# Joining two value parts in one product, and moving tiles and sparse steps between the stages of a decoder layer

## The chip, the cores and the metric

The kernel runs on one core of a Trainium2 chip. The metric is the device time of one execution in microseconds; shorter is better. TensorE is called PE, VectorE DVE, ScalarE ACT, GpSimd POOL and SyncE SP, as in the profile.

## The reference, cut to what matters

One decoder layer for 256 tokens of 1024 columns in float32: conditioned norm, an input projection with a retention group and a sparse-attention group, an output projection, and then an expert stage, in which the change lies:

```python
q = (hblk @ w_q).reshape(B, TB, PEER_HEADS, 2, PEER_DHALF)
s = jnp.einsum('btphd,phnd->btphn', q, subkeys).astype(jnp.float32)
v, i = lax.top_k(s, PEER_TOPK)
cand = (v[..., 0, :, None] + v[..., 1, None, :]).reshape(B, TB, PEER_HEADS, PEER_TOPK * PEER_TOPK)
cidx = (i[..., 0, :, None] * PEER_NKEYS + i[..., 1, None, :]).reshape(B, TB, PEER_HEADS, PEER_TOPK * PEER_TOPK)
tv, tj = lax.top_k(cand, PEER_TOPK)
eidx = jnp.take_along_axis(cidx, tj, axis=-1)
w = jax.nn.softmax(tv, axis=-1)
u = w_down[eidx]
a = jax.nn.gelu(jnp.einsum('btd,btpkd->btpk', hblk, u).astype(jnp.float32))
vv = w_up[eidx]
return jnp.einsum('btpk,btpkd->btd', (w * a).astype(hblk.dtype), vv)
```

Each token chooses 16 of 16384 experts for each of 8 heads, 128 expert numbers and weights in all. An expert is a row of `w_down` and a row of `w_up`.

## The kernel before, in words

The expert stage treats two sets of tokens differently. For the last 192 tokens (TD) it computes the whole 16384 x 192 table: 128 **down tiles** (one block of 128 experts each) give the Gelu of the down products, a **W part** writes the weights that the tokens give to the experts, and 128 **up units** multiply the weighted table with `w_up`. For the first 64 tokens (TS) it gathers the chosen rows: 64 **sparse steps** fetch 128 rows of `w_down` each with an indirect DMA on POOL (tile `row`, 0.5 MB) and take dot products on DVE, and 64 more fetch rows of `w_up` and add them up in `accS` (`sparse_gen`, lines 1028 to 1063).

The order of work is written out by the loop at line 1255. It walks a list `seq` of units: 16 query units (`wq`), then 128 down units; after the W part the rest of the down units alternate with up units, and the other up units follow. Beside the units run two generators:

- `gen` is first `top_gen` (line 941), which builds the expert lists on DVE, and then `w_gen` (line 1065). Each piece of it costs credits at its `yield`; each unit brings credits: CQ = 1.7 for a query unit, CT = 1.1 for a down unit while the lists are built (phase "top"), CD = 1.15 in the W part. So the credits decide how many tiles lie beside the lists and beside the W part. The lists cost 1.1 for each of 32 first-stage lists and 2 x (2 x 1.1 + 8 x 2.1 + 1.3 + 1.0) for the second stage of the two token blocks; the W part costs 1.0 + 0.4 for each of 48 groups. What is unspent is kept, up to 3.
- `spg` is the sparse work. A down unit brings it RD = 0.7 of a step, an up unit RU = 0.45.

A down tile (`down_unit`, line 1098) is done in one of two ways. A **wide** tile is split first (`split`): ACT copies the raw tile to `H` (float32r), DVE subtracts it to `L`, and PE multiplies 8 times `H` with 384 columns and `L` with 192; ACT then copies one half of the PSUM bank to `g` and DVE adds the other half. A **whole** tile goes to PE as plain float32, which the profile counts as 16 products of 192 columns, and needs neither split nor sum. `split_to` (line 1229) chooses: all tiles of phase "top" are whole, and every third one in the W part. In every case ACT then takes the Gelu from PSUM or `g`.

A W group (4 tokens) goes so: DVE compares a table of the token's expert numbers with a counting tile, which gives two one-hot tiles `o0` and `o1` (float16), and multiplies one of them with the weight's high part (`ow0`); ACT multiplies it with the low part, token by token (`ow1`, four instructions). PE adds up two products of 128 columns in one PSUM bank `w` for each token, eight in all, each with its own load of the same one-hot. After the next `yield`, tiles that are done already (`na` of them) are multiplied in place by DVE (`scalar_tensor_tensor`, which reads PSUM), in two halves VL and VH, and for those not yet done ACT copies the weights there, to be multiplied later.

PSUM has two `w` banks, two `dn` and four `acc`. Down tiles take `dn` or `acc` before the up part, and `dn` alone in it, since the up units' sums lie in `acc`. Raw tiles come by SP's queue, four units ahead, in four buffers; a wide tile frees its buffer after the split, a whole one after its products.

On ACT the Exp of the softmax (line 980) stands in `top_gen` once for each token block; the list indices and weights are then turned by PE (transposes at 1002 to 1004) and cast by DVE to the tables that the W part reads.

Of the kernel before, what the change touches and what calls it, by code (L numbers as in the profile page):

```python
# [24 lines left out]
F32 = mybir.dt.float32  # L25
F32R = mybir.dt.float32r
BF = mybir.dt.bfloat16
F16 = mybir.dt.float16
# [27 lines left out]
BLK = 8  # L56
BD = 3
WD = 3
RD = 0.7
RU = 0.45  # L60
EARLY = 5
NF1 = 3
NF2 = 1
FAFTER = False
SPL = 1
CT = 1.1
AFTER = ("top",)
NCAND = 50
CAND = [(0, 0, 1, 16), (16, 1, 2, 8), (24, 2, 3, 5), (29, 3, 4, 4), (33, 4, 5, 3), (36, 5, 8, 2), (42, 8, 16, 1)]
# [2 lines left out]
def build(tc, I, out, dbg=None, stop=None):  # L72
# [868 lines left out]
    def top_gen(sc):  # L941

        for i in range(16):
            while i not in sc:
                yield None
            b = sc.pop(i)
            for tt in range(2):
                top16(b[:, tt, :], tv1[tt][:, i, :], ti1[tt][:, i, :], P, "s2")
                yield 1.1
        for tt in range(2):  # L950
            fi = mk(tk, (P, 8, 2, 16), F32, "fi", bufs=2)
            V.tensor_copy(fi, ti1[tt].rearrange("p (a b) c -> p a b c", b=2))
            V.tensor_scalar(fi[:, :, 0, :], fi[:, :, 0, :], 128.0, None, op0=ALU.mult)
            v4 = tv1[tt].rearrange("p (a b) c -> p a b c", b=2)
            cand = mk(tk, (P, 8, NCAND), F32, "cand", bufs=2)
            cidx = mk(tk, (P, 8, NCAND), F32, "cidx", bufs=2)
            for src, dst in ((v4, cand), (fi, cidx)):
                for o, a0, a1, nb in CAND:
                    n = (a1 - a0) * nb
                    V.tensor_tensor(dst[:, :, o:o + n].rearrange("p h (a b) -> p h a b", b=nb),  # L960
                                    src[:, :, 0, a0:a1, None].to_broadcast([P, 8, a1 - a0, nb]),
                                    src[:, :, 1, None, 0:nb].to_broadcast([P, 8, a1 - a0, nb]), op=ALU.add)
                yield 1.1
            tv = mk(tk, (P, 8, 16), F32, "tv", bufs=2)
            tp = mk(tk, (P, 8, 16), U32, "tp", bufs=2)
            tpf = mk(tk, (P, 8, 16), BF, "tpf", bufs=2)
            ev = mk(tk, (P, 8, 16), F32, "ev", bufs=2)
            for p in range(8):
                top16(cand[:, p, :], tv[:, p, :], tp[:, p, :], NCAND, "s3")
                V.tensor_copy(tpf[:, p, :], tp[:, p, :])  # L970
                oh = mk(tk, (P, NCAND, 16), BF, "oh", bufs=1)
                V.tensor_tensor(oh, ioj, tpf[:, p:p + 1, :].to_broadcast([P, NCAND, 16]), op=ALU.is_equal)
                oe = mk(tk, (P, NCAND, 16), F32, "oe", bufs=2)
                V.tensor_tensor(oe, oh, cidx[:, p, :, None].to_broadcast([P, NCAND, 16]), op=ALU.mult)
                V.tensor_reduce(ev[:, p, :], oe.rearrange("p j k -> p k j"), axis=AX.X, op=ALU.add)
                yield 2.1

            ex = mk(tk, (P, 8, 16), F32, "ex", bufs=2)
            V.tensor_tensor(ex, tv, tv[:, :, 0:1].to_broadcast([P, 8, 16]), op=ALU.subtract)
            S.activation(ex, ex, AF.Exp)  # L980
            sm = mk(tk, (P, 8), F32, "smx", bufs=2)
            V.tensor_reduce(sm, ex, axis=AX.X, op=ALU.add)
            V.reciprocal(sm, sm)
            V.tensor_tensor(ex, ex, sm[:, :, None].to_broadcast([P, 8, 16]), op=ALU.mult)
            ei = mk(tk, (P, P), I32, "ei", bufs=2)
            V.tensor_copy(ei, ev.rearrange("p a b -> p (a b)"))
            e1 = mk(tk, (P, 2, P), I32, "e1", bufs=1)
            V.tensor_scalar(e1[:, 0, :], ei, 7, None, op0=ALU.arith_shift_right)
            V.tensor_scalar(e1[:, 1, :], ei, 127, None, op0=ALU.bitwise_and)
            ef = mk(tk, (P, 2, P), F32, "ef", bufs=1)  # L990
            V.tensor_copy(ef, e1)
            if tt == 0:

                ew = ex.rearrange("p a b -> p (a b)")
                V.tensor_copy(idxS[:TS, :], ei[:TS, :NJ])
                V.tensor_copy(wS[:TS, :], ew[:TS, :NJ])
                G.dma_start(idxS[TS:, :], ei[:TS, NJ:])
                last["G"] = G.dma_start(wS[TS:, :], ew[:TS, NJ:])
                spg.append(sparse_gen())
            yield 1.3  # L1000
            b = bank("w")[:, :3 * P].rearrange("p (a b) -> p a b", a=3)
            PE.transpose(b[:, 0, :], ef[:, 0, :], ident)
            PE.transpose(b[:, 1, :], ef[:, 1, :], ident)
            PE.transpose(b[:, 2, :], ex.rearrange("p a b -> p (a b)"), ident)
            tq = slice(tt * P, (tt + 1) * P)
            S.activation(tab[:, :, tq], b[:, 0:2, :], AF.Copy)
            wt = mk(tk, (P, P), F32, "wt", bufs=1)
            S.activation(wt, b[:, 2, :], AF.Copy, scale=WSC)
            dump(f"e{tt}", ev)
            dump(f"w{tt}", ex)  # L1010

            V.tensor_copy(tabw[:, tq], wt)
            V.tensor_tensor(tabl[:, tq], wt, tabw[:, tq], op=ALU.subtract)
            yield 1.0
# [50 lines left out]
    def w_gen(ohp):  # L1065

        half = NT // 2
        for gi in range(TD // 4):
            v0 = gi * 4
            t0 = TS + v0  # L1070
            oh = []
            for n in (1, 0):
                o = mk(ohp, (P, P, WG), F16, f"o{n}")
                V.tensor_tensor(o, iow, tab[:, n, None, t0:t0 + WG].to_broadcast([P, P, WG]), op=ALU.is_equal)
                oh.append(o)
            ow = [mk(ohp, (P, P, WG), F16, f"ow{n}") for n in range(2)]
            V.tensor_tensor(ow[0], oh[1], tabw[:, None, t0:t0 + WG].to_broadcast([P, P, WG]), op=ALU.mult)
            for t in range(WG):
                S.activation(ow[1][:, :, t], oh[1][:, :, t], AF.Copy, scale=tabl[:, t0 + t:t0 + t + 1])
            b = bank("w").rearrange("p (a b) -> p a b", a=4)  # L1080
            for t in range(WG):
                for n in range(2):
                    mm(b[:, t, :], oh[0][:, :, t], ow[n][:, :, t], n == 0, n == 1)
            yield 1.0
            bv = b.rearrange("p t i -> p i t")
            na = state["na"]
            for i0, buf in ((0, VL), (half, VH[0])):
                a = min(max(na - i0, 0), half)
                o = buf[:, :, v0:v0 + 4]
                if a:  # L1090
                    V.scalar_tensor_tensor(o[:, :a, :], bv[:, i0:i0 + a, :], 1.0 / WSC, o[:, :a, :], op0=ALU.mult,
                                           op1=ALU.mult)
                if a < half:
                    S.activation(o[:, a:, :], bv[:, i0 + a:i0 + half, :], AF.Copy, scale=1.0 / WSC)
            state["t0"] = v0 + 4
            yield 0.4

    def down_unit(n):
        wide = n not in whole
        if wide:  # L1100
            h, l = splits.pop(("down", n))
        else:
            r, _ = raws.pop(("down", n))
        b = bank("dn" if phase == "up" or n % 3 == 2 else "acc")[:, :2 * TD]
        for k in range(KC):
            ks = slice(k * P, (k + 1) * P)
            if wide:
                two = [(b.rearrange("p (a b) -> p a b", a=2), h[:, ks], h2[k // 4][:, k % 4, :, TS:]),
                       (b[:, :TD], l[:, ks], h2H[:, k, TS:])]
                for n_, o in enumerate(two[::-1] if k else two):  # L1110
                    mm(*o, k == 0 and n_ == 0, k == KC - 1 and n_ == 1)
            else:
                mm(b[:, :TD], r[:, ks], h2f[:, k, :], k == 0, k == KC - 1)
        t0 = state["t0"]
        v = vtile(n)
        if t0 or wide:
            g = mk(gt, (P, TD), F32, "g")
        src = b
        if wide:
            S.activation(g, b[:, TD:], AF.Copy)  # L1120
            V.tensor_tensor(g, g, b[:, :TD], op=ALU.add)
            src = g
        if t0 < TD:
            last["U"] = S.activation(v[:, t0:], src[:, t0:TD], AF.Gelu_apprx_tanh)
        if t0:
            S.activation(g[:, :t0], src[:, :t0], AF.Gelu_apprx_tanh)
            last["U"] = V.tensor_tensor(v[:, :t0], v[:, :t0], g[:, :t0], op=ALU.mult)
        state["na"] = n + 1
# [100 lines left out]
    def split_to(i):  # L1229
        while splitted[0] <= i and splitted[0] < len(seq):  # L1230
            u, n = seq[splitted[0]]
            if u == "down" and (phase == "top" or phase == "w" and n % WD == 0):
                whole.add(n)
                splitted[0] += 1
                continue
# [245 lines left out]
```

## Time and profile before

| | |
|---|---|
| median of 3 runs | 967.46 us (966.09 to 971.69) |
| profiled execution, its own time | 963.1 us |
| its span, first to last instruction | 960.9 us |
| PE busy | 905.5 us, 94% |
| DVE busy | 810.4 us, 84% |
| ACT busy | 521.2 us, 54% |
| POOL busy | 224.8 us, 23% |
| DMA | 266.43 MB, mean 277 GB/s |
| mean granted clock of PE | 0.979 |

A row of the profile names an engine, an operation and its tiles as out<-in with partitions x columns; then how often it ran (x), its busy time and the mean ns of one, and the idle time of the engine just before it with what ended it. Products overlap in PE, so that their durations add up to more than the time they take, and the same holds, by some 0.1 us, for DVE and ACT. Nearly all lines of the kernel go through one helper at line 88; the tiles tell the rows apart.

### The profile page before, as it was taken

How to read it: one execution, taken by the hardware profiler on the slowest of the kernel's cores; microseconds unless marked ns; L12 is line 12 of the kernel's file. 1: busy time of each engine (PE TensorE's matmuls, PEld its weight loads, DVE VectorE, ACT ScalarE, POOL GpSimd, SP SyncE). 2: the span in 40 equal slices, each digit the busy share in tenths (PEclk: the TensorE clock that was granted, in tenths of full speed). 3: DMA queues.
4: the chain of work that ended last, by engine and by line, in shares of the span. 5: the costliest groups of instructions: out<-in, count | busy, mean ns of one | idle time of the engine just before them, and what ended most of it. 6: DMA issues, size and time to landing. Idle time of an engine off the chain costs nothing.

```text
span 960.9 us, 15265 instructions
## 1 busy us (share of the span) xinstructions
PE 905.5 (94%) x5198; PEld 797.2 (83%) x5198; DVE 810.4 (84%) x1788; ACT 521.2 (54%) x1151; POOL 224.8 (23%) x172
## 2 busy tenths in 40 slices
PE   7999999999999799999989987899999989999994
PEld 6875667899999799999989986788887867888883
DVE  7988888689998922899998986889988979898887
ACT  7543697344221123778776754556564545555564
POOL 2040000110004200123223312334442425233311
PEclk9999999999999899999999988999999999999998
DMA  9978765354569976778777677899999999899981
GB/s 361 393 283 290 263 220 177 129 158 143 153 207 387 338 227 218 260 264 281 270 257 263 248 255 258 288 321 345 348 351 359 384 352 354 339 337 341 332 290 44
DMA packets 74749, 266.43 MB, mean 277 GB/s; under 512 B 9400, under 2 KB 9712, under 8 KB 74288
## 3 DMA queue, kind: packets, MB, share of 16 engines
q1 hardware_dynamic: 55200, 193.59, 57.5%
q0 software_dynamic: 19328, 71.61, 20.4%
q8 instruction: 41, 0.67, 0.3%
q14 instruction: 36, 0.29, 0.1%
q10 hardware_dynamic: 144, 0.26, 0.1%
HBM read 263.03 MB, written 2.11 MB: 276 GB/s over the span
## 4 chain that ended last, share of the span: by engine, by line
PE 51%; DVE 26%; DMA 8%; ACT 7%; issue 6%; POOL 1%; SPq 0%; DVEq 0%; ACTq 0%; POOLq 0%
PE acc L88 32%; DVE row L88 5%; PE C L88 5%; PE dn L88 4%; PE O L88 4%; DVE L L88 4%; PE S L88 3%; PE T L88 2%; DVE ev L88 2%; DVE o L88 2%; DMA row<-in_downN_dram,idxS 2%; ACT H L88 2%; ACT ow L88 1%; DMA raw<-in_down_dram 1%; DVE VL L88 1%
## 5 line engine op out<-in xcount | busy, mean ns | idle before, releaser
L88 DVE TENSOR_TENSOR L<-raw,H 128x1024 fp32r<-128x1024 f32 x216 | 263.2, 1220 | 41.9 <-ACT H L88 37.3
L88 ACT ACTIVATE H<-raw 128x1024 fp32r<-128x1024 f32 x216 | 228.2, 1058 | 122.2 <-DMA raw<-in_up_dram 73.4
L88 PE MATMUL acc<-H,a 128*128 128x512 f32 (+1 forms) x774 | 269.9, 397 | 4.4 <-DVE a L88 4.3
L88 PE MATMUL acc<-L,a 128*128 128x512 f32 (+1 forms) x515 | 203.4, 395 | 6.7 <-DVE L L88 6.7
L88 PEld LDWEIGHTS acc<-H,a 128*128 128x128 f32 x774 | 149.4, 193 | 39.8 <-DVE a L88 9.6
L1025 POOL DMA_INDIRECT row<-in_up_dram,idxS x64 | 116.2, 1815 | 196.2 <-DVE accS L88 163.8
L88 PE MATMUL acc<-h2f,raw 128*128 128x192 f32 x816 | 139.2, 326 | 0.0
L1025 POOL DMA_INDIRECT row<-in_downN_dram,idxS x64 | 77.5, 1210 | 242.6 <-DVE VH L88 85.4
L88 PEld LDWEIGHTS acc<-h2f,raw 128*128 128x128 f32 x816 | 133.0, 190 | 0.0
L88 PEld LDWEIGHTS acc<-L,a 128*128 128x128 f32 x515 | 99.1, 192 | 26.5 <-DVE L L88 7.1
L88 PE MATMUL dn<-hT,H 128*128 128x384 f32 x328 | 101.8, 367 | 5.4 <-DVE g L88 5.2
L88 PE MATMUL acc<-hT,H 128*128 128x256 f32 (+1 forms) x408 | 98.0, 323 | 3.6 <-ACT g L88 3.6
L88 DVE SCALAR_TENSOR_TENSOR row<-row,h2rep 128x1024 f32<-128x1024 f32 x64 | 77.9, 1218 | 8.8 <-DMA row<-in_downN_dram,idxS 8.6
L88 DVE SCALAR_TENSOR_TENSOR accS<-row,cS,accS 128x1024 f32<-128x1024 f32 x64 | 81.7, 1277 | 2.2 <-DMA row<-in_up_dram,idxS 2.2
L88 PE MATMUL dn<-hT,L 128*128 128x192 f32 x328 | 77.1, 255 | 0.0
L88 ACT ACTIVATE ow<-o,VL 128x128 f16<-128x128 f16 x192 | 74.4, 572 | 4.0 <-DVE o L88 3.4
L88 PEld LDWEIGHTS acc<-hT,H 128*128 128x128 f32 x408 | 69.7, 194 | 3.9 <-ACT g L88 3.9
L88 PE MATMUL acc<-hT,L 128*128 128x192 f32 (+1 forms) x280 | 72.5, 270 | 0.0
L88 PEld LDWEIGHTS dn<-hT,H 128*128 128x128 f32 x328 | 62.5, 191 | 8.5 <-DVE g L88 7.3
L88 PEld LDWEIGHTS dn<-hT,L 128*128 128x128 f32 x328 | 62.8, 193 | 0.7
L88 PE MATMUL w<-ow,o 128*128 128x128 f16 x384 | 53.2, 296 | 4.1 <-DVE ow L88 2.5
L88 PE MATMUL dn<-h2f,raw 128*128 128x192 f32 x272 | 48.5, 333 | 6.3 <-ACT VL L88 6.3
(355 smaller groups left out, 1367.2 us busy)
## 6 DMA issues: line engine op xcount, KB each, us to landing
raw<-in_down_dram SPq DMA_DIRECT2D x128, 512.0 KB, 4.3
raw<-in_up_dram SPq DMA_DIRECT2D x128, 512.0 KB, 6.3
adaraw<-in_wadaT_dram SPq DMA_DIRECT2D x40, 512.0 KB, 6.0
raw<-in_wq_dram SPq DMA_DIRECT2D x16, 512.0 KB, 3.5
raw<-in_win_C_dram SPq DMA_DIRECT2D x12, 512.0 KB, 6.3
rawA<-in_win_A_dram SPq DMA_DIRECT2D x8, 512.0 KB, 6.5
raw<-in_wout_dram SPq DMA_DIRECT2D x8, 512.0 KB, 3.7
VL<-in_wadaT_dram SPq DMA_DIRECT2D x8, 512.0 KB, 7.1
```

The lines of the kernel that those rows point to most:

```text
L88: i = fn(*a, **kw)
L1025: G.indirect_dma_start(r, None, src, bass.IndirectOffsetOnAxis(ap=idxS[:, j:j + 1], axis=0))
```

## The change

The W group loads the one-hot of a token once and multiplies it with both value parts side by side (256 columns), so that the parts stand next to each other in PSUM and not summed; two tokens fill a bank, a group both `w` banks. ACT copies the low part with the scale to a new tile `wl`, DVE adds the scaled high part to it, and the later multiplication reads `wl` in SBUF. CT rises from 1.1 to 1.5, RD from 0.7 to 0.9, and RU falls from 0.45 to 0.3. In the W part two tiles of three are whole where it was one of three, in the up part every other one where it was none, and down tiles of the up part take `dn` and `w` banks in turn. The Exp of the softmax is ordered behind the last down tile's Gelu.

```diff
@@ -56,14 +56,14 @@
 BLK = 8
 BD = 3
 WD = 3
-RD = 0.7
-RU = 0.45
+RD = 0.9
+RU = 0.3
 EARLY = 5
 NF1 = 3
 NF2 = 1
 FAFTER = False
 SPL = 1
-CT = 1.1
+CT = 1.5
 AFTER = ("top",)
 NCAND = 50
 CAND = [(0, 0, 1, 16), (16, 1, 2, 8), (24, 2, 3, 5), (29, 3, 4, 4), (33, 4, 5, 3), (36, 5, 8, 2), (42, 8, 16, 1)]
@@ -977,7 +977,8 @@
 
             ex = mk(tk, (P, 8, 16), F32, "ex", bufs=2)
             V.tensor_tensor(ex, tv, tv[:, :, 0:1].to_broadcast([P, 8, 16]), op=ALU.subtract)
-            S.activation(ex, ex, AF.Exp)
+            with (tc.issue_after(last["U"].ins) if "U" in last else ExitStack()):
+                S.activation(ex, ex, AF.Exp)
             sm = mk(tk, (P, 8), F32, "smx", bufs=2)
             V.tensor_reduce(sm, ex, axis=AX.X, op=ALU.add)
             V.reciprocal(sm, sm)
@@ -1073,25 +1074,32 @@
                 o = mk(ohp, (P, P, WG), F16, f"o{n}")
                 V.tensor_tensor(o, iow, tab[:, n, None, t0:t0 + WG].to_broadcast([P, P, WG]), op=ALU.is_equal)
                 oh.append(o)
-            ow = [mk(ohp, (P, P, WG), F16, f"ow{n}") for n in range(2)]
-            V.tensor_tensor(ow[0], oh[1], tabw[:, None, t0:t0 + WG].to_broadcast([P, P, WG]), op=ALU.mult)
+            ow = mk(ohp, (P, 2, P, WG), F16, "ow")
+            V.tensor_tensor(ow[:, 0], oh[1], tabw[:, None, t0:t0 + WG].to_broadcast([P, P, WG]), op=ALU.mult)
             for t in range(WG):
-                S.activation(ow[1][:, :, t], oh[1][:, :, t], AF.Copy, scale=tabl[:, t0 + t:t0 + t + 1])
-            b = bank("w").rearrange("p (a b) -> p a b", a=4)
-            for t in range(WG):
-                for n in range(2):
-                    mm(b[:, t, :], oh[0][:, :, t], ow[n][:, :, t], n == 0, n == 1)
+                S.activation(ow[:, 1, :, t], oh[1][:, :, t], AF.Copy, scale=tabl[:, t0 + t:t0 + t + 1])
+            bs = []
+            for t in range(0, WG, 2):
+                b = bank("w").rearrange("p (t n i) -> p t n i", t=2, n=2)
+                for q in range(2):
+                    mm(b[:, q], oh[0][:, :, t + q], ow[:, :, :, t + q], True, True)
+                bs.append(b)
             yield 1.0
-            bv = b.rearrange("p t i -> p i t")
+
+            wl = mk(ohp, (P, WG, P), F32, "wl", bufs=1)
+            for t, b in enumerate(bs):
+                x = wl[:, 2 * t:2 * t + 2, :]
+                S.activation(x, b[:, :, 1, :], AF.Copy, scale=1.0 / WSC)
+                V.scalar_tensor_tensor(x, b[:, :, 0, :], 1.0 / WSC, x, op0=ALU.mult, op1=ALU.add)
+            bv = wl.rearrange("p t i -> p i t")
             na = state["na"]
             for i0, buf in ((0, VL), (half, VH[0])):
                 a = min(max(na - i0, 0), half)
                 o = buf[:, :, v0:v0 + 4]
                 if a:
-                    V.scalar_tensor_tensor(o[:, :a, :], bv[:, i0:i0 + a, :], 1.0 / WSC, o[:, :a, :], op0=ALU.mult,
-                                           op1=ALU.mult)
+                    V.tensor_tensor(o[:, :a, :], bv[:, i0:i0 + a, :], o[:, :a, :], op=ALU.mult)
                 if a < half:
-                    S.activation(o[:, a:, :], bv[:, i0 + a:i0 + half, :], AF.Copy, scale=1.0 / WSC)
+                    S.activation(o[:, a:, :], bv[:, i0 + a:i0 + half, :], AF.Copy)
             state["t0"] = v0 + 4
             yield 0.4
 
@@ -1101,7 +1109,7 @@
             h, l = splits.pop(("down", n))
         else:
             r, _ = raws.pop(("down", n))
-        b = bank("dn" if phase == "up" or n % 3 == 2 else "acc")[:, :2 * TD]
+        b = bank(("dn" if n % 2 else "w") if phase == "up" else "dn" if n % 3 == 2 else "acc")[:, :2 * TD]
         for k in range(KC):
             ks = slice(k * P, (k + 1) * P)
             if wide:
@@ -1229,7 +1237,7 @@
     def split_to(i):
         while splitted[0] <= i and splitted[0] < len(seq):
             u, n = seq[splitted[0]]
-            if u == "down" and (phase == "top" or phase == "w" and n % WD == 0):
+            if u == "down" and (phase == "top" or n % (WD if phase == "w" else 2)):
                 whole.add(n)
                 splitted[0] += 1
                 continue
```

## Rows read from the trace of the kernel before

**Rows 1.** Busy time in stretches; columns PE, weight loads, DVE, ACT, POOL, clock, DMA, GB/s.

```profile
334.00:376.00 42.00, 41.74 (x251) 41.66 (x252) 7.64 (x25) 10.18 (x35) 2.04 (x3) 0.96 0.69 214
376.00:570.00 194.00, 186.07 (x1292) 180.82 (x1290) 176.81 (x427) 145.32 (x436) 47.92 (x38) 0.97 0.78 265
440.00:460.00 20.00, 20.00 (x144) 19.51 (x144) 19.46 (x50) 15.30 (x46) 6.07 (x5) 1.00 0.83 279
```

**Rows 2.** Timeline of DVE around the end of the top part; start, us, instruction.

```profile
336.31 0.29 DVE L88 CAST ef<-e 128x256 f32<-128x256 int32 x1
...
341.48 0.43 DVE L88 TENSOR_TENSOR o<-VL 128x512 f16<-128x512 f16 x1 [0.95 <-ACT ow L88]
...
373.31 0.23 DVE L88 CAST VL<-wt 128x128 f16<-128x128 f32 x1 [21.09 <-ACT wt L88]
```

**Rows 3.** Timeline of PE over the same stretch.

```profile
334.26 4.30 PE L88 MATMUL dn<-h2f,raw 128*128 128x192 f32 x16 [6.27 <-ACT VL L88]
...
372.20 0.38 PE L88 MATMUL w<-ident,ef 128*128 128x128 f32 x2
...
375.13 1.11 PE L88 MATMUL w<-ow,o 128*128 128x128 f16 x8
```

**Rows 4.** Timeline of ACT over the same stretch.

```profile
330.96 1.28 ACT L88 ACT_TABLE_LOAD   x1 [21.14 <-DVE ex L88]
```

**Rows 5.** Groups of instructions of the W part, 376 to 570 us; last column idle before.

```profile
L88 PE MATMUL acc<-h2f,raw 128*128 128x192 f32 x304 | 53.0, 327 | 0.0
...
L88 PE MATMUL acc<-hT,H 128*128 128x384 f32 x152 | 50.1, 384 | 3.6 <-ACT g L88 3.6
...
L88 DVE TENSOR_TENSOR L<-raw,H 128x1024 fp32r<-128x1024 f32 x39 | 47.5, 1218 | 4.2 <-ACT H L88 4.2
L88 DVE SCALAR_TENSOR_TENSOR row<-row,h2rep 128x1024 f32<-128x1024 f32 x38 | 46.2, 1217 | 0.0
L88 PE MATMUL dn<-hT,H 128*128 128x384 f32 x145 | 46.2, 373 | 0.2 <-ACT VH L88 0.2
L88 ACT ACTIVATE H<-raw 128x1024 fp32r<-128x1024 f32 x40 | 42.5, 1062 | 3.8 <-DMA raw<-in_down_dram 3.8
```

**Rows 6.** Timeline of all engines in the W part.

```profile
439.82 0.35 DVE L88 TENSOR_TENSOR g<-g,dn 128x192 f32<-128x192 f32 x1
...
440.08 0.42 DVE L88 SCALAR_TENSOR_TENSOR VL<-w,VL 128x256 f32<-128x256 f32 x1
...
440.42 0.41 DVE L88 TENSOR_TENSOR o<-VL 128x512 f16<-128x512 f16 x1
...
441.22 1.22 DVE L88 SCALAR_TENSOR_TENSOR row<-row,h2rep 128x1024 f32<-128x1024 f32 x1
...
442.12 0.82 PEld L88 LDWEIGHTS <-o 128*128 128x128 f16 x8
...
442.44 1.21 DVE L88 TENSOR_TENSOR L<-raw,H 128x1024 fp32r<-128x1024 f32 x1
442.56 0.38 ACT L88 ACTIVATE VH<-w 128x248 f32<-128x248 f32 x1 [0.21 <-DVE VH L88]
...
443.57 0.22 DVE L88 TENSOR_TENSOR VH<-VH,g 128x64 f32<-128x64 f32 x1
```

**Rows 7.** The chain of waits, its long pieces: start, us, what.

```profile
214.13 2.87 PE acc L88 x24
...
338.56 5.20 PE acc L88 x32
...
564.45 4.65 PE acc L88 x16
...
677.54 2.28 PE dn L88 x16
...
848.87 95.98 PE acc L88 x416
```

**Rows 8.** Groups of the up part, 570 to 684 us.

```profile
L88 PE MATMUL dn<-hT,H 128*128 128x384 f32 x183 | 55.7, 362 | 5.2 <-DVE g L88 5.2
```

## The prediction

> **What bounds the kernel now.** I read the busy time in stretches first, then the timelines where an engine stands still, then the groups of one stretch for counts, and the chain for prices. Three parts matter. In the top part VectorE (DVE) builds the expert lists while TensorE (PE) works off plain down tiles. DVE has its last list at 336.3 us, does the first one-hots of the W part, and then stands from 341.9 to 373.3 us but for one scrap of work, because the second pair of transposes sits in PE's order behind a backlog of tiles and comes at 372.2 [rows 2, 3]: of 42 us DVE works 7.6 [rows 1]. PE lost time just before, 6.3 us, since ScalarE (ACT) had parked 21.1 us on the softmax's Exp, with the Gelus that free the PSUM banks queued behind it [rows 3, 4]. In the W part (first w product at 375.1 us) both are near full: PE 186.1 and DVE 176.8 of 194 us, and in its best stretch DVE does 19.46 of 20 us, 97% [rows 1]. In the up part PE is the bound: 128 up units at 95.98/416 = 0.231 us a product, ten products each, are 2.31 us each [rows 7].
>
> **Prices.** Where instructions overlap I take start to next start. A whole (plain float32) tile costs PE 5.20/2 = 2.60 us, a wide (split) one 2.28 [rows 7]. A wide tile costs DVE its L, 442.44 to 443.57 = 1.13, and the sum into g, 0.26; a sparse step costs 1.22 with its accumulator read; a 128x256 scalar_tensor_tensor that reads PSUM costs 0.34 [rows 6].
>
> **The schedule** follows from the credits. Top costs 77.8, of which the 16 query units pay 27.2; the rest is 46 to 47 tiles at 1.1 and 34 to 35 at 1.5. W costs 48 x 1.4 = 67.2, 58 tiles at 1.15 in both. So W covers tiles 47 to 104 before, 35 to 92 after, and 12 tiles move behind W. Wide tiles: before 38 in W (the rows show 297/8 = 37 [rows 5]) and 22 after it; after the change 19 and 18, with 17 whole ones in the up part. Sparse steps done when W starts and ends: 15 and 55 before (38 of them in the window [rows 5]); 14 and 66 after.
>
> **Top.** The second transposes come 12 x 2.60 = 31.2 us earlier on PE, at 341.0, or 334.7 if the 6.3 us also go because Exp now stands behind a Gelu; the list that they need is there at 336.6. I take W's DVE work to start at 337 (its first 16 groups need only the first token block's tables, so 341 would cost DVE little). Exp still waits for DVE, and what is behind it on ACT is the Gelus that PE's banks need: PE may wait some 6 us here as before, but DVE does not.
>
> **W, on DVE.** Before: 176.8 us in the window, and 2.7 us of one-hots that ran ahead. Added: two scalar_tensor_tensor a group that join the value parts, 96 x 0.34 = 32.6; 12 sparse steps more, 14.6. Removed: 19 wide tiles, 19 x 1.39 = 26.4; and since fewer tiles are done while W runs (a mean of 63 for 75), 4 us of the final multiplications, an estimate from 48 elements fewer and 10 second halves fewer. That is 196.3. At 95% busy, between the 91% of the whole W part and the 97% of its best stretch [rows 1], it takes 206.6 us, to 543.6.
>
> **W, on the others.** PE does 39 x 2.60 + 19 x 2.28 and 48 groups. A group's eight products took 0.82 [rows 6]; the four of twice the columns are nearest to the query units, where 24 pairs of a load and a 256-column product took 2.87, 0.12 each [rows 7], so 0.48 a group; bounds 0.43 (no load seen) and 0.82 (no gain). In sum 168 us of 207: the one load for each token saves PE 16 us where PE is no longer the bound, and I count nothing for it: DVE's 207 us hide it, and would hide the loss of it. ACT gains 96 copies of at most 0.38 [rows 6], 36 us, loses 19 splits of 1.06 [rows 5] and 19 copies, 27 us: 145 of 194 [rows 1] becomes 154 of 207, hidden by DVE as long as no copy comes late (rival 1 is what it costs if one does). POOL has 48 us of gathers in 194 [rows 1]; 12 more fit. SP issues the same loads.
>
> **Up part.** Before: 570.0 to 944.85 is 374.9 us; 23 wide tiles (183/8 [rows 8]), one whole and 128 ups make 350.7; so 24 us of waiting, much of it on DVE's g [rows 8]: a pair of a down and an up asked DVE for 2 x 1.13 + 3 x 0.26 + 1.15 x 1.22 = 4.4 of PE's 4.59 us. After: 18 x 2.28 + 17 x 2.60 + 295.7 = 380.9. A pair asks DVE for 1.13 + half of 1.39 + 2 x 0.26 + 1.2 x 1.22 = 3.8 of 4.75, and four PSUM banks serve the downs instead of two. I take 13 us of waiting, half; bounds 5 and 24. Bytes stay level in the pairs (3.2 loads and gathers of 0.52 MB in 4.75 us, 353 GB/s; 360 before) and fall behind them.
>
> **Sum.** 337 + 206.6 + 380.9 + 13 = 937.5, and the tail from 944.85 to the end of the span (16.05) unchanged: 953.6 for 960.9, so 7.3 us less. The profiled execution took 963.1 us, 4.4 under the median of the runs, 967.46; the forecast is 967.46 - 7.3 = 960.2.
>
> **Rivals.** (1) *Round trip in W* (slower). A group now fills both w banks, so the next group's products wait for ACT's copy and DVE's join of the last. For it: ACT already waits for DVE at its share of the evacuation [rows 6]. Against: DVE's own order puts the join before the next one-hots, and PE has 19% to spare. Price: each 0.1 us a group that DVE cannot fill is 4.8 us. The point of decision is 0.15 us a group; at 0.35, DVE falls to about 88% and the time is 960.2 + 17 = 977. The Trainium skill (Perfetto Trace Analysis, Optimizing Tensor Performance, Matmuls) says independent product groups should rotate through banks so that one's evacuation overlaps the next one's products, which speaks against this change; no row here shows a group that holds both banks. (2) *Clock* (slower). PE waits a little in every W group, and after the long wait before 564.45 a wide tile took 4.65 for 2.28 us [rows 7]. If a share f of W's tiles runs at that rate, PE's work of 168 passes 207 from f = 0.23; at 0.35 it costs 20 us, 980. Against: W's clock is 0.97 on average now, 1.00 in the stretch shown [rows 1]. The Trainium skill (TensorE: Matmul & The Clock Gate, A second HAM failure mode: psum-queue depth-cycling) tells of a kernel whose short pauses between groups kept switching the clock; the 1.2 GHz level shows here only behind long waits. (3) *More comes back*: DVE at 97% in W and 5 us of waiting later, 202.4 and 385.9, 12.2 less than the sum: 948. (4) *No change*: W at 93% (211.1) and 16 us of waiting later give 7.5 back: 967.7. That the planner would not move tiles can't be: the counts are fixed by the credits.
>
> **Chances.** Forecast (950 to 965) 0.42, of which 0.32 is a gain of over 0.5%; (3) 0.20, all of it one; (4) 0.18, most of it within 0.5%; (1) 0.13 and (2) 0.07, nearly all slower. A measurement of this kernel can tell about 0.5%, 4.8 us, from no change. So faster 0.52, the same 0.26, slower 0.22: the sum is small beside its unknowns, which are DVE's share in W (91 to 97%, 13 us) and the waiting after it (19 us). The range is 946 to 975; the forecast's own is 950 to 965.
>
> **What would show it.** Right: first w product near 340 us, DVE without its 30 us hole; W ending near 545 with DVE at 95% and PE near 81%; the last down tile some 160 us after that (31 pairs of 4.75 and the tiles ahead of them); fewer waits on g. Wrong: W longer than 215 us, PE's clock under 0.95 there, ACT waiting on the joins for tens of us, or W's first product still behind 350 us.

## The result, and the profile after

The changed kernel takes **1000.03 us** (median of 4 runs, 996.50 to 1004.88) against 968.79 of the kernel before (4 runs, 966.09 to 971.69): a ratio of 1.0328, with a 95% interval of 1.0287 to 1.037. It is slower, where a gain of 7 us was forecast, and it lies outside the range. The profiled execution took 1004.88 us, with a span of 1003.1.

The page of after, its busy shares (94% PE, 84% DVE and 54% ACT before) and the shares of the chain that ended last:

```profile
PE 921.9 (92%) x5004; PEld 796.4 (79%) x5006; DVE 823.4 (82%) x1840; ACT 538.3 (54%) x1212; POOL 194.1 (19%) x172
...
PE 52%; DVE 19%; DMA 16%; ACT 7%; issue 5%; POOL 1%; SPq 0%; DVEq 0%; ACTq 0%; POOLq 0%
```

The chain of before:

```profile
PE 51%; DVE 26%; DMA 8%; ACT 7%; issue 6%; POOL 1%; SPq 0%; DVEq 0%; ACTq 0%; POOLq 0%
```

No engine is busier than before in its share: 42 us more of span hold 16 us more of PE's busy time. So the time went into waiting, and on the chain loads (DMA) hold 16% for 8%. Busy time of after in three stretches: the W part, the **alternating stretch** (down tiles and up units by turns, to the end of the last down tile), and the up units alone, almost to their end; columns as in [rows 1]:

```profile
357.30:566.10 208.80, 193.78 (x1096) 171.79 (x1095) 199.38 (x494) 165.56 (x504) 49.23 (x49) 0.97 0.80 266
566.10:753.60 187.50, 171.59 (x896) 155.47 (x895) 136.42 (x190) 78.14 (x145) 61.47 (x44) 0.95 0.87 307
753.60:985.00 231.40, 226.08 (x959) 184.25 (x958) 179.02 (x235) 128.18 (x195) 35.14 (x23) 0.99 0.82 289
```

Against the prediction's sum: the first W product at 357.3 for 337, **20.3 late**; W 208.8 for 206.6, 2.2 more; from there to the end of the up part 420.5 for 393.9, **26.6 more**; the tail 16.5 for 16.05. These are 49.5 us, the whole way from 953.6 to 1003.1. The end of the up part is taken as the prediction took it, from the chain's last long piece, here to 986.63 us:

```profile
861.49 125.14 PE acc L88 x541
```

**The 20 us** are seen on three engines. PE, by its timeline of after (compare [rows 3]):

```profile
294.45 0.38 PE L88 MATMUL w<-ident,ef 128*128 128x128 f32 x2
...
317.52 0.48 PE L88 MATMUL w<-ident,ex 128*128 128x128 f32 x1 [20.73 <-DVE ex L88]
...
354.02 0.38 PE L88 MATMUL w<-ident,ef 128*128 128x128 f32 x2
...
357.28 1.08 PE L88 MATMUL w<-ow,o 128*128 128x256 f16 x4
...
464.48 1.08 PE L88 MATMUL w<-ow,o 128*128 128x256 f16 x4
465.38 0.83 PE L88 MATMUL dn<-h2f,raw 128*128 128x192 f32 x4
```

The first block's transposes come at 294.45, and the third of them needs `ex`, which is 20.7 us late; PE stands with all tiles queued behind it. ACT, over the same time (compare [rows 4]):

```profile
293.69 0.31 ACT L88 ACTIVATE ex<-ex 128x128 f32<-128x128 f32 x1
...
318.03 0.38 ACT L88 ACTIVATE VL<-w 128x256 f16<-128x256 f32 x1 [22.38 <-PE w L88]
...
353.26 0.31 ACT L88 ACTIVATE ex<-ex 128x128 f32<-128x128 f32 x1
```

Exp no longer blocks ACT: it runs at 293.69, behind the Gelus that PE had ready. But what follows from it runs on DVE (compare [rows 2]):

```profile
314.56 0.28 DVE L88 TENSOR_REDUCE smx<-ex 128x8 f32<-128x128 f32 x1
...
317.18 0.28 DVE L88 TENSOR_TENSOR ex<-ex,smx 128x128 f32<-128x128 f32 x1
...
344.28 0.17 DVE L88 TENSOR_TENSOR cS<-cS,wS 128x8 f32<-128x8 f32 x1 [4.68 <-ACT cS L88]
...
353.60 0.29 DVE L88 TENSOR_REDUCE smx<-ex 128x8 f32<-128x128 f32 x1 [9.16 <-ACT ex L88]
```

Exp ended at 294.00 and its sum began at 314.56, without DVE waiting for it: in DVE's order the sum stands behind some 20 us of the second block's lists and of sparse steps. In the second block the sum waits 9.2 us for an Exp that stands behind the Gelus of PE's backlog. So DVE's hole before W, which the change was to close, is smaller and not gone: 13.8 us in two pieces for 31.

**The 27 us** lie in the up part, most of them in the alternating stretch; 4.2 us of them are 1.6 whole tiles of the W part, which PE did behind the last W product. Waits of after from 566.1 to 753.6 us; columns: total us, times, longest:

```profile
DVE L L88 <- ACT H L88: 45.2, 22, 5.7
ACT H L88 <- DMA raw<-in_up_dram: 41.4, 17, 6.7
...
PE dn L88 <- DVE g L88: 10.1, 4, 3.5
```

A load of up rows is late, ACT waits to split it, DVE waits for ACT, and then PE waits for a sum that DVE does behind it. One such chain, by the timeline of all engines (SPq is SP's DMA queue):

```profile
667.97 0.42 SPq L88 DMA_DIRECT2D raw<-in_up_dram  x1
...
673.84 1.06 ACT L88 ACTIVATE H<-raw 128x1024 fp32r<-128x1024 f32 x1 [6.43 <-DMA raw<-in_up_dram]
...
674.92 1.22 DVE L88 TENSOR_TENSOR L<-raw,H 128x1024 fp32r<-128x1024 f32 x1 [5.67 <-ACT H L88]
...
676.74 4.36 PE L88 MATMUL dn<-h2f,raw 128*128 128x192 f32 x16 [2.79 <-DVE g L88]
```

The whole tile after the wait took 4.36 us where its price is 2.60, and the stretch's granted clock is 0.95.

The W part kept its length, but not its parts. Groups of the W part of after, by form; columns as in [rows 5]:

```profile
L88 DVE SCALAR_TENSOR_TENSOR row<-row,h2rep 128x1024 f32<-128x1024 f32 x49 | 59.8, 1220 | 0.0
...
L88 PE MATMUL w<-ow,o 128*128 128x256 f16 x192 | 54.3, 403 | 15.0 <-DVE ow L88 10.4 <-DVE wl L88 3.3 <-DVE o L88 0.7
...
L88 DVE SCALAR_TENSOR_TENSOR wl<-w,wl 128x256 f32<-128x256 f32 x94 | 36.2, 419 | 1.6 <-ACT wl L88 1.2
...
L88 DVE TENSOR_TENSOR L<-raw,H 128x1024 fp32r<-128x1024 f32 x20 | 24.4, 1220 | 3.0 <-ACT H L88 2.7
...
L88 ACT ACTIVATE VH<-wl 128x256 f32<-128x256 f32 x25 | 16.3, 652 | 0.0
L88 DVE TENSOR_TENSOR VL<-wl,VL 128x256 f32<-128x256 f32 x22 | 13.3, 605 | 0.1
```

The joins are 94 and cost 36 us of DVE, and the four products of a group take 465.38 - 464.48 = 0.90 us, as the eight did before (from the last group's first product at 568.88 to PE's next instruction at 569.78 us).

### The profile page after: what moved, and what is told of

The parts are those of the page before. It is cut to its first block, busy times and chain, and to the rows that moved or that the text cites. A ratio compares the mean times of both kernels' runs of the same rounds, so it can differ in the third digit from the quotient of the medians.

```text
span 1003.1 us, 14967 instructions
## 1 busy us (share of the span) xinstructions
PE 921.9 (92%) x5004; PEld 796.4 (79%) x5006; DVE 823.4 (82%) x1840; ACT 538.3 (54%) x1212; POOL 194.1 (19%) x172
## 4 chain that ended last, share of the span: by engine, by line
PE 52%; DVE 19%; DMA 16%; ACT 7%; issue 5%; POOL 1%; SPq 0%; DVEq 0%; ACTq 0%; POOLq 0%
PE acc L88 29%; PE dn L88 7%; DMA raw<-in_up_dram 5%; PE C L88 4%; DMA raw<-in_down_dram 4%; DMA VL<-in_wadaT_dram 4%; PE w L88 4%; DVE L L88 4%; DVE row L88 3%; PE O L88 3%; PE S L88 2%; PE T L88 2%; DVE VL L88 2%; ACT H L88 2%; DVE wl L88 1%
## 5 line engine op out<-in xcount | busy, mean ns | idle before, releaser
L88 DVE TENSOR_TENSOR L<-raw,H 128x1024 fp32r<-128x1024 f32 x193 | 235.4, 1221 | 91.2 <-ACT H L88 65.5
L88 ACT ACTIVATE H<-raw 128x1024 fp32r<-128x1024 f32 x193 | 204.4, 1061 | 184.7 <-PE acc L88 85.9
L88 PE MATMUL acc<-H,a 128*128 128x512 f32 (+1 forms) x774 | 273.7, 400 | 10.4 <-DVE a L88 5.3
L88 PE MATMUL dn<-h2f,raw 128*128 128x192 f32 x768 | 142.9, 339 | 10.3 <-DVE g L88 10.1
L88 PEld LDWEIGHTS dn<-h2f,raw 128*128 128x128 f32 x768 | 134.5, 200 | 16.6 <-DVE g L88 12.2
L1026 POOL DMA_INDIRECT row<-in_up_dram,idxS x64 | 96.5, 1507 | 240.3 <-DVE accS L88 206.7
L88 PE MATMUL acc<-h2f,raw 128*128 128x192 f32 x688 | 120.7, 332 | 0.0
L88 PE MATMUL w<-ow,o 128*128 128x256 f16 x192 | 54.3, 403 | 15.0 <-DVE ow L88 10.4
L88 PEld LDWEIGHTS acc<-hT,L 128*128 128x128 f32 x280 | 55.9, 200 | 1.2 <-issue 0.2
L88 DVE SCALAR_TENSOR_TENSOR adaraw<-adaraw,cs 128x1024 f32<-128x1024 f32 x40 | 48.5, 1217 | 0.0
L88 PEld LDWEIGHTS <-o 128*128 128x128 f16 x192 | 19.6, 118 | 29.3 <-DVE ow L88 12.8
```

The source lines that it names most:

```text
L88: i = fn(*a, **kw)
L1026: G.indirect_dma_start(r, None, src, bass.IndirectOffsetOnAxis(ap=idxS[:, j:j + 1], axis=0))
```

## The experiments

All are set against the kernel before, which had medians of 967.13, 966.43 and 966.99 us in the three sets of runs. The theory: the Exp's order costs some 20 us, the joins cost DVE time in W for nothing in return, and the alternating stretch waits by what its pairs of a tile and an up unit ask for, and so longer the more tiles are moved into it. "Waiting" in that stretch is its length less what its units cost by the prediction's prices; a table behind the last experiment has it for all runs with 35 or more tiles there.

**1. The change without the Exp's order.**

```diff
-            with (tc.issue_after(last["U"].ins) if "U" in last else ExitStack()):
-                S.activation(ex, ex, AF.Exp)
+            S.activation(ex, ex, AF.Exp)
```

> The changed kernel with the Exp's order behind the Gelu taken back, nothing else. Theory (the order makes the softmax's sums come late on DVE, PE stands 20.7 us at the first turned weights and DVE stands 14 us at the second ones): the PE wait at 296 to 317 us goes, the first w product comes at 338 to 343 us instead of 357, and the time falls by 14 to 20 us, to 980 to 986. Rival (PE's backlog of tiles sets the start of the W part whatever the Exp does): the first w product stays within 5 us of 357 and the time within 5 us of 1000.

Measured: 979.79 us (974.43 to 984.34), ratio 1.0131 [1.0074, 1.0188], 20.2 us less than the changed kernel. PE's timeline:

```profile
294.80 0.27 PE L88 MATMUL w<-ident,ex 128*128 128x128 f32 x1
...
341.02 0.27 PE L88 MATMUL w<-ident,ex 128*128 128x128 f32 x1
...
343.73 1.08 PE L88 MATMUL w<-ow,o 128*128 128x256 f16 x4
```

The third transpose follows at once, the second ones come at 341.0 as the prediction had it without the 6.3 us, and W starts 13.6 us earlier. The rest of the gain lies behind W's start, most of it in the alternating stretch (180.6 us for 187.5); why that stretch is shorter too isn't shown.

**2. The Exp's order alone**, in the kernel before (the reverse of that diff).

> The kernel before with the Exp ordered behind the last down tile's Gelu, nothing else. Theory: the first sums of the softmax fall behind the second block's lists on DVE, PE meets the first turned weights with nothing to do and stands 15 to 25 us, the backlog after it comes as much later, time 980 to 992. Rival (the parked ACT of 21 us is what costs, and the order cures it): 6 us less, 962.

Measured: 983.75 us (978.94 to 987.66), ratio 1.0152 [1.011, 1.0194], as the theory has it; the first W product comes at 390.8 for 375.1. The order costs 16 to 20 us in either kernel, by the same wait: PE's timeline of this run.

```profile
313.71 0.38 PE L88 MATMUL w<-ident,ef 128*128 128x128 f32 x2
335.19 0.47 PE L88 MATMUL w<-ident,ex 128*128 128x128 f32 x1 [21.10 <-DVE ex L88]
```

**3. The joined products alone**: the kernel before with the W group of the change (its hunk of `w_gen`), all else as before.

> The kernel before with the joined value products alone (one load for each token, two banks for a group, ACT's copy and DVE's sum), its schedule unchanged. Theory (DVE bounds the W part, so its 32.6 us more come through and PE's 16 us less do not): W part 20 to 33 us longer than 195, time 985 to 1000. Rival (PE's saving pays for it): time within 8 us of 968.

Measured: 999.25 us (996.38 to 1001.3), ratio 1.0319 [1.0279, 1.0359]. W takes 231.2 us for 194.7, and DVE is busy for 215.5 of them, 39 us more than before in [rows 1]: the joins (33) and the slower reading of `wl` (below). The time is within what the theory gave; W is 36.5 us longer where it gave 20 to 33. PE waits 18.0 us for `wl` there, and the granted clock of the part is 0.92 for 0.97, so a few of the 36.5 us may be theirs.

**4. The change without the Exp's order and without the joins**: beside the first diff, the old products and the old multiplication from PSUM.

```diff
-            ow = mk(ohp, (P, 2, P, WG), F16, "ow")
+            ow = [mk(ohp, (P, P, WG), F16, f"ow{n}") for n in range(2)]
...
-                    mm(b[:, q], oh[0][:, :, t + q], ow[:, :, :, t + q], True, True)
+                for n in range(2):
+                    mm(b[:, t, :], oh[0][:, :, t], ow[n][:, :, t], n == 0, n == 1)
...
-                V.scalar_tensor_tensor(x, b[:, :, 0, :], 1.0 / WSC, x, op0=ALU.mult, op1=ALU.add)
```

> The changed kernel with the Exp's order taken back, and the W groups written as before (two one-hot loads and two added products for each token, no join on DVE). Theory (the joins on DVE set W's length, and the spared loads on PE are worth nothing): DVE loses 33 to 40 us of joins, W falls from 207.1 us until PE is the bound: 39 whole tiles x 2.60 + 19 wide x 2.28 + 48 x 0.82 = 184 us, so W 184 to 190 us, and the time 979.8 - 17 to 23, which is 957 to 963 (up to 968 if the later stretch gives some back). Rival (the joins are not what bounds W; the load of a one-hot on PE or ACT's copies are): W stays at 200 us or more and the time at 973 or more.

Measured: **957.7 us** (956.41 to 962.24), ratio 0.9923 [0.9893, 0.9953], 22 us less than experiment 1 and faster than before. Its W part and its alternating stretch:

```profile
343.60:528.90 185.30, 185.30 (x1283) 181.66 (x1281) 163.16 (x401) 130.25 (x409) 50.45 (x49) 1.00 0.85 299
528.90:708.00 179.10, 167.06 (x903) 151.01 (x902) 136.06 (x188) 78.51 (x146) 62.89 (x45) 0.98 0.90 323
```

PE is busy for all 185.3 us of W, at a clock of 1.00, and DVE for 163.2. So the moved tiles and sparse steps were worth 9 us; the joins and the Exp's order took 42.

**5. Half of the moves alone**: the kernel before with CT = 1.5.

> The kernel before with CT = 1.5 alone (12 tiles of the top part moved behind the W part). Theory (DVE's hole of 31 us goes, the W part starts at 340 to 344 us, but the pairs of a down and an up, 31 for 19, wait as much each as before): 955 to 965. Rival (the whole hole comes through): 936 to 945. Rival (moved tiles cost as much as the hole): 967 or more.

Measured: 964.0 us (959.85 to 968.4, 10 runs), ratio 0.9978 [0.9952, 1.0004], which can't be told from no change. W starts at 343.5 and ends at 533.5, 36 us earlier than before; the alternating stretch with its 12 more tiles takes 180.0 us for 114.7, and the rest 246 for 276. The hole before W is closed, W is 5 us shorter, and all of it but some 2 us is given back later, 27 us of it as the own work of 12 tiles that is only moved (12 x 2.28) and some 8 as waiting in the stretch (24 us for 16), about as much for each pair as before.

**6. All tiles of the up part wide**, in the changed kernel.

```diff
-            if u == "down" and (phase == "top" or n % (WD if phase == "w" else 2)):
+            if u == "down" and (phase == "top" or phase == "w" and n % WD):
```

> The changed kernel with all down tiles of the up part wide (split) again, the banks in turn and the sparse rates as in the change. Theory (a whole tile keeps its raw buffer until PE is done with it, so that the next loads are issued late and PE waits for them in the up part): up part 25 us shorter, of which 5 are PE's cheaper tiles, time 973 to 982. Rival (the waiting there comes from the denser sparse gathers or the banks in turn): the part stays within 8 us and the time at 992 to 1000.

Measured: 987.37 us (986.06 to 988.27), ratio 1.0205 [1.017, 1.0239]: 12.7 us less than the changed kernel, between the two figures. DVE, with 160.6 of 175.8 us in the alternating stretch, has little left there.

**7. Experiments 1 and 6 together.**

> The changed kernel with the Exp's order taken back and all down tiles of the up part wide. Theory (the two costs add: 20 us and 13 us measured one by one): 1000 - 33 = 967, 962 to 972. Rival (they share a cause, the late start of the W part): 975 to 980.

Measured: 978.41 us (971.2 to 984.79), ratio 1.0114 [1.004, 1.0187]. The theory's sum of the two gains did not come: with the Exp freed, wide tiles change nothing that can be measured (978.41 for 979.79). With wide tiles the alternating stretch is 175.8 us in experiment 6 and 176.8 here; with whole ones it is 187.5 in the changed kernel and 180.6 in experiment 1. So it is the stretch with whole tiles that differs between its runs (187.5 again in experiment 10, 179.1 in experiment 4), and why is open. The waits in the alternating stretch have changed their kind, though:

```profile
ACT g L88 <- DVE g L88: 19.0, 15, 2.8
ACT H L88 <- DMA raw<-in_down_dram: 16.5, 12, 2.1
...
DVE L L88 <- ACT H L88: 12.8, 23, 1.6
```

The late up loads (39.5 us of ACT's time in experiment 1) are gone from the list, and waits for DVE's `g` stand in their place, as before [rows 8]; DVE is busy for 160.5 of 176.8 us. With whole tiles the loads come late, with wide ones DVE does, and PE loses as much.

**8. Thin sparse work in the alternating stretch**, beside experiment 1.

```diff
-            scred += RU if u == "up" else RD
+            scred += RD if phase != "up" else 0.3 if any(w == "down" for w, _ in seq[i:i + 2]) else 0.45
```

> The changed kernel with the Exp's order taken back (as in the first of these runs, 980 us) and half the sparse steps beside the pairs of a down and an up (0.6 a pair for 1.2), the rest beside the up units alone (0.45 for 0.3). Theory (a whole tile holds its raw buffer, so the loads are late whatever the gathers do): the pairs' stretch stays at 172 to 182 us, time 975 to 985. Rival (the gathers crowd the loads): the stretch falls to 160 to 166 us and the time to 963 to 970.

Measured: 968.65 us (964.06 to 974.55, 10 runs), ratio 1.0017 [0.9989, 1.0044], 11 us less than experiment 1. The alternating stretch of experiment 1, and then of this one:

```profile
551.00:731.60 180.60, 167.10 (x898) 151.49 (x897) 138.86 (x193) 79.16 (x147) 62.20 (x45) 0.97 0.90 321
```

```profile
549.70:721.00 171.30, 164.66 (x898) 150.12 (x896) 116.85 (x174) 79.58 (x147) 35.45 (x25) 0.98 0.80 277
```

20 gathers fewer, 277 GB/s for 321, and the waits of ACT for up loads fall from 39.5 to 24.9 us. By the prices of the units (31 ups of 2.31, 18.6 whole and 18 wide tiles: 161.0) the waiting falls from 20 to 10 us. The time is the rival's, and the stretch lies between what the theory and the rival gave.

**9. The same with all tiles of the up part wide**, to see whether the remaining waiting comes from whole tiles, which hold their raw buffers until their products are done.

> The changed kernel with the Exp's order taken back, all tiles of the up part wide, and thinner sparse work while tiles and up units alternate (0.3 of a step a unit, then 0.45). Theory (what was left of the waiting with thin sparse work, 171.5 us for the alternating stretch, comes from whole tiles that hold their raw buffers until their products are done): the stretch falls to 160 us or less, and the time to 956 to 963. Rival (the rest is DVE's own work for a pair and the start of the stretch): with wide tiles DVE has more to do, the stretch stays at 166 to 174 us and the time at 964 to 972.

Measured: 962.15 us (960.95 to 963.89), ratio 0.995 [0.9929, 0.997]. The alternating stretch:

```profile
550.50:716.30 165.80, 160.71 (x898) 144.54 (x897) 139.22 (x205) 99.36 (x179) 37.32 (x26) 0.98 0.84 285
```

It is 5.5 us shorter than in experiment 8, and 17 tiles at 2.28 for 2.60 are 5.4 us of that. So the waiting is the same (10 us). The held buffers do make the up loads late (those waits of ACT fall from 24.9 to 5.3 us), but that is not what is left of PE's waiting: that part of the theory falls, though the time lies where it was put. More raw buffers, a direct test, weren't tried.

**10. The sparse rates of before**, beside experiment 1. The kernel that ran differs from the text below in two points: it has RD = 0.7 and RU = 0.45 throughout, and every other tile of the up part is still whole.

```diff
-RD = 0.9
-RU = 0.3
+RD = 0.7
+RU = 0.45
```

> The changed kernel with the Exp's order taken back, 0.7 of a sparse step for a tile (40 steps in W in place of 52), 0.3 for each unit while tiles and up units alternate, 0.45 for an up unit behind the last tile, and all tiles of the up part wide. Theory (W pays a sparse step with 1.22 us of DVE at 95%, and up units alone have room for it): W 207.1 - 15 = 192 us, the stretch of alternating units as with the wide tiles before (176 to 178), and the rest, from the last tile to the end, no longer than 250: 964 to 970. Rival (a step costs the same wherever it lies): W 192, the rest longer by the same 12 to 15 us (257 or more), and the time 976 or more.

Measured: 979.7 us (977.91 to 985.69), ratio 1.015 [1.0108, 1.0192], level with experiment 1. W falls by 7.6 us, to 199.7, where 12 steps fewer were to save 15; the alternating stretch grows by 7, to 187.5, at nearly the same pace of sparse steps (1.15 for 1.2 a pair). What W gives, the stretch takes, as the rival has it for a later place; but since the kernel is not the one described, it decides nothing between the two, and why the stretch grew isn't shown.

**11. Sparse work later, in the kernel before**: CT = 1.5, RD = 0.5, RU = 0.6.

> The kernel before with CT = 1.5, RD = 0.5 and RU = 0.6: the tiles move as in the change, the sparse steps the other way, out of the W part (29 there for 40 before and 52 in the change) into the part of up units alone, where DVE had room. Theory (DVE bounds the W part and not the up units): W part 180 to 185 us for 195, time 930 to 948. Rival (the gathers make the loads of the up part late, which the change avoided): 960 to 975.

Measured: 955.61 us (950.9 to 957.42), ratio 0.988 [0.9832, 0.9928]: a gain, but smaller than forecast. W takes 183 us, of which PE is busy for 180.7; the alternating stretch is still 174.3, and the up units alone move 354 GB/s.

**12. Sparse work later, and thin in the alternating stretch, in the kernel before.**

```diff
-RD = 0.7
-RU = 0.45
+RD = 0.6
+RU = 0.65
...
-CT = 1.1
+CT = 1.5
...
-            scred += RU if u == "up" else RD
+            scred += RD if phase != "up" else 0.35 if any(w == "down" for w, _ in seq[i:i + 2]) else RU
```

> The kernel before with 1.5 credits for a tile of the top part, 0.6 of a sparse step for a down tile, 0.35 for each unit while tiles and up units alternate, and 0.65 for an up unit behind the last tile: the sparse work is moved away from the alternating stretch. Theory (sparse work costs where DVE and the loads are near full and is free behind the last tile): W 186 us, the alternating stretch 168 us or less, the rest 250: 945 to 955. Rival (the transfers bound the end: up units alone already move some 380 GB/s): the rest grows to 258 or more, and the time is 956 to 963.

Measured: **951.69 us** (949.89 to 954.09), ratio 0.9852 [0.9829, 0.9875]; it beats both kernels. Its three stretches:

```profile
338.50:525.40 186.90, 182.57 (x1286) 177.77 (x1285) 167.93 (x403) 147.63 (x446) 37.17 (x32) 0.99 0.75 253
525.40:692.10 166.70, 160.38 (x900) 145.14 (x898) 139.88 (x229) 98.90 (x179) 46.51 (x29) 0.98 0.83 293
692.10:931.00 238.90, 230.82 (x966) 181.68 (x965) 219.72 (x272) 130.57 (x196) 109.29 (x60) 1.00 0.94 362
```

The up units alone take the sparse work at 362 GB/s, and from the last tile to the span's end it is 255 us, as in experiment 11 and some 8 more than in the other kernels with this many up units left: the price of it, smaller than what the stretch before saves.

The alternating stretch in the runs side by side. The tiles are those that PE does in it, with what is left of W's last tiles; the waiting is the length less the units (ups 2.31, 19 of them before and 31 in the others; whole tiles 2.60, wide ones 2.28):

| run | sparse steps a pair | whole tiles | wide tiles | length, us | waiting, us |
|---|---|---|---|---|---|
| before | 1.15 | 1 | 23 | 114.7 | 16 |
| after | 1.2 | 18.6 | 18 | 187.5 | 26.5 |
| 10 | 1.15 | 19 | 18 | 187.5 | 25 |
| 5 | 1.15 | 1 | 35.7 | 180.0 | 24 |
| 7 | 1.2 | 1.6 | 35 | 176.8 | 21 |
| 6 | 1.2 | 1.6 | 35 | 175.8 | 20 |
| 1 | 1.2 | 18.6 | 18 | 180.6 | 20 |
| 11 | 1.1 | 1 | 35.9 | 174.3 | 18 |
| 4 | 1.2 | 19 | 18 | 179.1 | 17 |
| 12 | 0.7 | 1 | 35.7 | 166.7 | 11 |
| 8 | 0.6 | 18.6 | 18 | 171.3 | 10 |
| 9 | 0.6 | 1.6 | 35 | 165.8 | 10 |

## Why the prediction was wrong

- **Top: the step that failed first** is "Exp still waits for DVE ... PE may wait some 6 us here as before, but DVE does not". It followed Exp on ACT's queue only. Exp's followers (the sum, its reciprocal, the product) stand on DVE, and with Exp late they came to stand behind the second block's lists, so PE waited 20.7 us for them. Undone it gives 20.2 us (experiment 1), 13.6 of them at W's start; done alone it costs 16 to 17 (experiment 2). Without the order W begins at 343.7, not at 337: the second transposes come at 341.0, as the prediction had them with the 6.3 us of PE's waiting still there, and the first product 2.7 us behind them. These are the other 6.7 of the 20.3 us. "W's first product still behind 350 us" was named as a sign against, and it came.
- **Up part: the term mis-sized** is "I take 13 us of waiting, half; bounds 5 and 24". It was 35, above the upper bound: 26.5 in the alternating stretch and 9 behind it (the last 4 of the 39.6 us over the units' 380.9 are the 1.6 tiles that the sum had counted in W alone). The prediction took the waiting for DVE's alone and halved it because whole tiles ask DVE for less. They do, but then the up loads came late, and PE waited as long (20 us in experiment 1 with whole tiles, 21 in experiment 7 with wide ones). And it halved a total, where 16 of the 24 us before lay in the alternating stretch and recurred with each pair: 16 us on the 19 pairs of before are 16/19 x 31 = 26 on 31, which is what the changed kernel shows; the 9 us behind the stretch stayed. What sets the waiting is what DVE and the loads share, the sparse steps: at 1.1 to 1.2 a pair the kernels with the longer stretch wait 17 to 27 us there, whole or wide, and at 0.6 or 0.7 they wait 10 or 11; experiment 8 changes nothing else beside experiment 1 in that stretch. The "four PSUM banks" for the downs seem to have done little: experiments 5 and 7, with two and with four, wait 24 and 21 us, though they differ in the W part too.
- **W: its length was right, 208.8 for 206.6**, and DVE's share was 95% as taken. PE was not: 194 us for 168. "0.48 a group" was priced by the query units; measured is 0.90, above the upper bound of 0.82, so 48 groups cost 20 us more. (The 0.82 of [rows 6] is the time of the eight loads; the eight products took 0.90 from start to next start.) At a granted clock of 0.97 the tiles also took longer than their prices. It cost nothing only because DVE was the bound. The joins at 0.34, 33 us in sum, fit DVE's 199.4 us for the 196.3 of the sum.
- **What the sum said of the joins stands**: they add 33 us to DVE and take nothing from the path. The runs sharpen it: alone they cost 32 us, taken out they give 22, since PE then is the bound at 185.3 us. That the change as a whole still came out ahead in the forecast rested on closing DVE's hole of 31 us. Without the Exp's order W does start 31.4 us earlier (343.7 for 375.1); the order took back 13.6 of these, and 20 us of the whole time.
- **Rivals.** (1) The round trip in W: PE waited 3.3 us on `wl` and 10.4 on `ow`, and DVE kept 95%; it did not happen. The Trainium skill (Perfetto Trace Analysis, Optimizing Tensor Performance, Matmuls) has independent groups rotate through banks; holding both banks for a group cost little here, by those 3.3 us, and more in experiment 3, where PE waited 18.0 us for `wl` and DVE's share was 93%. (2) The clock in W was 0.97, as before. The loss of clock was in the alternating stretch, 0.95, behind its waits. (3) and (4) erred on the same two terms as the forecast. No rival had the Exp's followers on DVE.
- **The direction of the sparse steps** was costed as 14.6 us in W and a smaller stretch later. Experiments 11 and 12 show the other direction to be the better: W loses them, the units alone take them.

## What to carry to other kernels

When an instruction is moved on one engine, follow its result over every engine down to the next one that stands still: here an order put on ACT delayed three small DVE instructions by 20 us, and through them PE. A wait that recurs with each pair of units is priced for each pair and multiplied by the new number of pairs; half of an old total is no estimate. And joining products to save PE's time pays only where PE is the bound and where the joined form is shorter by a row of the same access pattern.

## What the runs showed of the hardware

- Four products of 256 float16 columns took 0.90 us, the same as eight of 128: 0.22 us for 256 columns, where the query units' 256 take 0.12 [rows 7]. The one-hots' columns lie four elements apart (4 tokens side by side), the query units' next to each other. That the spacing is the cause is likely, but wasn't tried by itself, and the operands' type differs too.
- `wl` lies in SBUF with the columns read 512 bytes apart. DVE's product from it took 605 ns for 128x256 where the one from PSUM in the same order took 0.42 us [rows 6], and ACT's copy 652 ns for 0.38 us. The Trainium skill (SBUF — State Buffer, Door 1: The DMA port swizzle) says that reads which cross to a new line of 16 bytes each time pay a penalty. The trace agrees: the reads at 512 bytes took 1.4 times as long on DVE and 1.7 on ACT as those from PSUM, and the join, which takes `wl` in the order in which it lies, took 419 ns. DVE's product from PSUM was another operation (it scaled as well), so its factor is not the reading's alone.
